# Gates of a retrieval layer as two float16 pieces instead of three bf16 ones, and kept in DRAM with eight keys side by side instead of four

## The chip, the cores and the metric

The kernel runs on one core of a Trainium2 chip. Its time is the device time of one launch in microseconds. The engines of the core are named as the profile names them: PE (TensorE, matmuls; PEld is its weight load), DVE (VectorE), ACT (ScalarE), POOL (GpSimd), SP (the queue that issues most DMAs). Each of them works through its own list of instructions in order and waits on semaphores that the others set.

## What is computed

The reference is one decoder block on 512 tokens of width 1024: a mixer (a recurrent group of heads beside sliding-window attention), then a layer that retrieves experts, then a final norm. The change touches the retrieval layer only. Cut to what matters:

```python
def block(x_b):                                  # x_b: a block of tokens, h after the norm
    q = (x_b @ wq).reshape(-1, H, 2, PEER_HALF)  # 8 heads, two half queries
    s = einsum('thcd,hcnd->thcn', q, subkeys)    # 128 scores for each half
    s_top, i_top = top_k(s, 16)
    cand_s = s_top[:, :, 0, :, None] + s_top[:, :, 1, None, :]
    cand_i = i_top[:, :, 0, :, None] * 128 + i_top[:, :, 1, None, :]
    best_s, best_pos = top_k(cand_s, 16)
    idx = take(cand_i, best_pos)                 # 8 x 16 experts for a token
    gate = softmax(best_s)
    act = gelu(einsum('td,ted->te', x_b, u_tab[idx]))
    return einsum('te,ted->td', gate * act, v_tab[idx])
```

There are 128 x 128 experts, each named by a pair of keys.

## The kernel before

**Two ways for the tokens.** The first 128 tokens gather their 128 expert rows each from the tables (indirect DMAs on POOL, line 1079; the dot products and sums on DVE, lines 1092 and 1090). The other 384 tokens (ND) are done densely: for each of 128 blocks b (one value of one key; the 128 values of the other key lie on the partitions) the kernel multiplies all 128 experts of the block with all 384 tokens (`up_product`, 24 matmuls of 384 columns at lines 173 to 175, since every operand is split into a high and a low part), takes the Gelu (`up_act`, line 886), multiplies by a dense matrix of gates that is zero where an expert was not chosen (`weigh`, line 1218, on POOL) and adds the product with the block's value rows into six PSUM banks (`accumulate`, lines 1263 to 1265).

**The gates.** The dense gates are made ahead of the main loop, in 96 steps n of four tokens each, 8 steps to a group of TC = 32 tokens, 32 steps to a tile of 128 tokens. At the start of a tile `chosen(t)` transposes the gates and both keys of the 128 chosen slots (line 1109), copies the gates to `rest` (1115) and the keys to `sK` (1117), and takes the gates apart into bf16 pieces `sG`: a cast on ACT (1119), and between two casts a subtraction on DVE (1121), three casts and two subtractions. For each step `one_hots(n)`, called three steps ahead, makes on DVE the tile `O` (1136: for four tokens the one-hot rows of both keys, 1024 elements) and `P` (1141: the one-hot row of one key times each of the three pieces, 1536 elements). PE then multiplies O with P (1163): for each of four tokens three matmuls of 128 columns, added up in PSUM as `pG`. ACT copies `pG` to the staging tile `gst` (1164). After 8 steps one DMA writes `gst`, 2 MB, to DRAM (`gates`, 1173). In DRAM a partition's GI x TC numbers for GI = 4 blocks b lie side by side, 512 bytes; the last group of 32 tokens is written in eight parts (1173 and 1242).

**What else lies between.** A fixed order is written out by hand (`manual_schedule`): during the 96 steps the program also runs 34 `up_product`s ahead (each in two halves, by `steps(ups, ...)`), with `up_split` (a cast on ACT, line 163, and a subtraction on DVE, line 164, that make `uh` and `ul`), the load of the next `u` block (`up_load`, 783), and 44 of the gathers with their DVE work. Then, after the last gates are written, `gate_load` (1202) reads the gates back, 12 DMAs of 64 KB for four blocks b, and the main loop over 128 blocks begins.

Of the kernel before, what the change touches and what calls it, by code (L numbers as in the profile page):

```python
# [6 lines left out]

F32 = mybir.dt.float32
F32R = mybir.dt.float32r
BF = mybir.dt.bfloat16  # L10
I32 = mybir.dt.int32
U32 = mybir.dt.uint32
AF = mybir.ActivationFunctionType
# [33 lines left out]
AHEAD = 2  # L47

LASTG = 120
ND = 384  # L50
CH0 = 512 - ND
NCAND = [min(16, 16 // (a + 1)) for a in range(16)]
# [21 lines left out]
def _emit(ctx, tc, A, out, dbg, stop):  # L74
    nc = tc.nc
    V, SC, PE, GP, SY = nc.vector, nc.scalar, nc.tensor, nc.gpsimd, nc.sync
    mm = PE.matmul
# [109 lines left out]
    def pt(tag, name, shape=(128, 512)):  # L187
        return ps.tile(list(shape), F32, name=name, tag=tag, bufs=2)
# [16 lines left out]
    def rms(pool, n, width, name, add_eng):  # L205


        acc = pool.tile([128, S], F32, name=name + "acc")
        rs = consts.tile([128, NT], F32, name=name + "rs")

        def take(k, src):
            if k == 0:
                SC.activation(acc, src, AF.Square)
                return
            sq = pool.tile([128, S], F32, name=name + "sq", tag="rsq", bufs=3)
            SC.activation(sq, src, AF.Square)
            (V if k == n - 1 else add_eng).tensor_tensor(out=acc, in0=acc, in1=sq, op=OP.add)

        def scale():
            pss = pt("att", name + "ss", (128, NT))  # L220
            for t in range(NT):
                mm(pss[:, t:t + 1], acc[:, t * 128:(t + 1) * 128], ones[:, 0:1], start=True, stop=True)
            rsqrt(rs, pss, NT, 1.0 / width, RMS_EPS)
            return rs

        def spread():
            pb = pt("att", name + "b")
            for t in range(NT):
                mm(pb[:, t * 128:(t + 1) * 128], rs[:, t:t + 1].to_broadcast([128, 128]), ident,
                   start=True, stop=True)  # L230
            return pb

        return take, scale, spread


    take, scale, spread = rms(xp, KD, D, "n1", V)
# [528 lines left out]
    mpst, mp = right("mp")  # L765
# [4 lines left out]
    iota = mp.tile([128, 128], F32, name="iota")  # L770
    GP.iota(iota, pattern=[[1, 128]], base=0, channel_multiplier=0, allow_small_or_imprecise_dtypes=True)

    iota2 = mp.tile([128, 128, 2], BF, name="iota2")
    GP.iota(iota2, pattern=[[1, 128], [0, 2]], base=0, channel_multiplier=0, allow_small_or_imprecise_dtypes=True)

    pust, pool_u = right("pu", 2)
# [37 lines left out]
    take, scale, spread = rms(x2p, KD, D, "n2", GP)  # L814
    for i in range(KD):
        whi, wlo = load_w(A["w_out"][i])
        p = pt(("proj", "chain")[i % 2], "pj")
# [27 lines left out]
    for k in range(KD):  # L845
        p = pt("tinv", "px2", (128, NT, 128))
# [67 lines left out]
    tk = tkst.enter_context(tc.tile_pool(name="tk", bufs=1, side="right", reuse_waits="tile"))  # L914
# [113 lines left out]
    for hc in range(16):  # L1028
# [8 lines left out]
        p = psT.tile([128, 512], F32, name="pq", tag="pq", bufs=2)  # L1037
# [5 lines left out]
        p = psT.tile([128, NT, 128], F32, name="psc", tag="psc", bufs=2)  # L1043
# [26 lines left out]
    tk = tkst.enter_context(tc.tile_pool(name="oh", bufs=1, side="right", reuse_waits="tile"))  # L1070
# [12 lines left out]
    def gathered(j):  # L1083
# [7 lines left out]
        else:  # L1091
            V.scalar_tensor_tensor(scr, r_, 1.0, h2g, op0=OP.mult, op1=OP.mult, accum_out=ac[:, jj:jj + 1])  # L1092

    TC, GI = 32, 4
    NG = 128 // GI
    NTC = ND // TC

    NG0 = 4
    gd = [[nc.dram_tensor(f"gates{t}_{g0}", (n, 128, GI * TC), F32, kind="Internal").ap() for g0, n in
           (((0, NG0), (NG0, NG - NG0)) if t == NTC - 1 else ((0, NG),))] for t in range(NTC)]  # L1100
    hot = {}

    def chosen(t):

        sK = tk.tile([128, 64, 2, 2], BF, name="sK", tag="sK", bufs=2)
        sG = tk.tile([128, 64, 3, 2], BF, name="sG", tag="sG", bufs=2)
        p = psT.tile([128, 3, 128], F32, name="psT", tag="sel", bufs=2)
        for i in range(3):
            PE.transpose(p[:, i, :], sg_[:, i, t].rearrange("p h s -> p (h s)"), ident)
        rest = tk.tile([128, 64, 2], F32, name="rest", tag="rest")  # L1110

        def pairs(x):
            return x.rearrange("p (n t) -> p n t", t=2)

        SC.copy(rest, pairs(p[:, 0]))
        for i in range(2):
            SC.copy(sK[:, :, i], pairs(p[:, 1 + i]))
        for i in range(3):
            SC.copy(sG[:, :, i], rest)
            if i < 2:  # L1120
                V.tensor_tensor(out=rest, in0=rest, in1=sG[:, :, i], op=OP.subtract)
        hot["s"] = sK, sG

    def one_hots(n):

        t, t0 = CH0 // 128 + n // 32, n % 32 * 4
        if t >= NT:
            return
        if t0 == 0:
            chosen(t)  # L1130
        sK, sG = hot["s"]
        ts = slice(t0 // 2, t0 // 2 + 2)

        O = tk.tile([128, 2, 2, 256], BF, name="O", tag="O", bufs=3)
        P = tk.tile([128, 2, 3, 256], BF, name="P", tag="P", bufs=3)
        V.tensor_tensor(out=O.rearrange("p n i (e t) -> p (n i) e t", t=2),  # L1136
                        in0=iota2[:, None].to_broadcast([128, 4, 128, 2]),
                        in1=sK[:, ts].rearrange("p n i t -> p (n i) t")[:, :, None, :].to_broadcast([128, 4, 128, 2]),
                        op=OP.is_equal)
        B5 = [128, 2, 3, 128, 2]  # L1140
        V.tensor_tensor(out=P.rearrange("p n i (e t) -> p n i e t", t=2),  # L1141
                        in0=O[:, :, 1:2].rearrange("p n i (e t) -> p n i e t", t=2).to_broadcast(B5),
                        in1=sG[:, ts, :, None, :].to_broadcast(B5), op=OP.mult)
        hot[n] = [x.rearrange("p n i (e t) -> p n i e t", t=2) for x in (O, P)]

    V.scalar_tensor_tensor(h2g, x2[:, 0, :], rs2[:, 0:1], ln2r, op0=OP.mult, op1=OP.mult)
    for n in range(3):
        one_hots(n)
    def pieces(ci):
        return ([(0, NG0)] + [(g, 4) for g in range(NG0, NG, 4)]) if ci == NTC - 1 else [(0, NG)]  # L1150

    done = asked = 0
    left = 2 * len(AHEAD_UP) - sum(UPS1) - sum(UPST) - BEHIND
    for n in range(8 * NTC):
        one_hots(n + 3)
        O, P = hot.pop(n)
        ci, t4 = n // 8, n % 8
        if t4 == 0:
            gst = tk.tile([128, NG, GI, TC], F32, name="gst", tag="gst", bufs=2)
        p = psT.tile([128, 4, 128], F32, name="pG", tag=("sel", "pq", "psc")[n % 3], bufs=2)  # L1160
        for u in range(4):
            for i in range(3):
                mm(p[:, u, :], O[:, u // 2, 0, :, u % 2], P[:, u // 2, i, :, u % 2], start=i == 0, stop=i == 2)  # L1163
        SC.copy(gst[:, :, :, t4 * 4:t4 * 4 + 4].rearrange("p n g t -> p (n g) t"), p.rearrange("p t e -> p e t"))  # L1164
        if t4 == 7:

            writes = []
            for g0, n_ in pieces(ci):
                d = gd[ci][g0 >= NG0 and ci == NTC - 1]
                d0 = NG0 if d.shape[0] == NG - NG0 else 0  # L1170
                writes.append((d[g0 - d0:g0 - d0 + n_].rearrange("n p x -> p n x"),
                               gst[:, g0:g0 + n_].rearrange("p n g t -> p n (g t)")))
            SY.dma_start(*writes.pop(0))
        steps(ups, (n + 1) * left // (8 * NTC) - n * left // (8 * NTC))
        while asked < (n + 1) * EARLY // (8 * NTC):
# [16 lines left out]
    def upto(b):  # L1192

        return min(256, EARLY + (256 - EARLY) * sum(cost[:b + 1]) // sum(cost[:LASTG + 1]))

    vs, ws, gts = {}, {}, {}

    def gate_load(g):
        gts[g] = pv_.tile([128, NTC, GI, TC], F32, name="gts", tag="gts", bufs=2)
        for i in range(NTC):  # L1200
            d, n = (gd[i][0], g) if len(gd[i]) == 1 or g < NG0 else (gd[i][1], g - NG0)
            SY.dma_start(gts[g][:, i], d[n].rearrange("p (g t) -> p g t", t=TC))  # L1202

    def load(b):
        if b >= 128:
# [86 lines left out]
    for b in range(127):  # L1292
# [10 lines left out]
        n = RING + b  # L1303
# [11 lines left out]
        for j in range(done, n1):  # L1315
            gather(j)
        if b > LASTG:
            steps(ends[0], 1)
# [74 lines left out]
```

## Time and profile before

| | |
|---|---|
| median of 3 runs | 1682.41 us (1679.21 to 1683.79) |
| the profiled execution's own time | 1679.72 us |
| its span | 1678.0 us |
| PE busy | 1607.2 us, 96% |
| DVE busy | 1305.7 us, 78% |
| ACT busy | 656.5 us, 39% |
| POOL busy | 712.4 us, 42% |
| the 96 gate steps | from about 601 us to 844 us of the span |

The span is the time from the first to the last instruction of the profiled execution; 1.7 us of its time lie around it. The busy times are unions of an engine's instructions; the end of a matmul is modelled, so a busy PE may still be waiting for a few ns in between. A row of a group gives how many instructions it holds, their busy time, the mean length of one, and the idle time ahead of them with what ended it.

### The profile page before, as it was taken

What the parts mean: (1) busy time and instruction counts of PE and PEld (TensorE: products, weight loads), DVE (VectorE), ACT (ScalarE), POOL (GpSimd) and SP (SyncE); (2) the same over time, 40 slices, a digit from 0 to 9 for tenths busy, and PEclk for the clock granted to TensorE, in tenths of its full rate; (3) what the DMA queues carried; (4) which work ended last, traced back from release to release, by engine and by line L of the source; (5) the groups of instructions that cost most, each with busy time, mean ns of one, the idle gap of its engine ahead of it and who ended that gap; (6) DMA issues with size and microseconds to landing.
All of it is one profiled execution on the core that took longest, in us unless ns stands there. A gap on an engine that the chain in (4) does not pass through costs nothing.

```text
span 1678.0 us, 30955 instructions
## 1 busy us (share of the span) xinstructions
PE 1607.2 (96%) x12013; PEld 1386.1 (83%) x12013; DVE 1305.7 (78%) x2477; ACT 656.5 (39%) x1081; POOL 712.4 (42%) x670
## 2 busy tenths in 40 slices
PE   5999999898999989989999999999999999999997
PEld 4777677676888889888889888888888888888886
DVE  5656448745799889999958777877878877788797
ACT  5444345533343434444443333333333333333334
POOL 5112110034676512121216565556565556556582
PEclk9999999999999999999999999999999999999999
DMA  4111110141222249898989989989888989889784
GB/s 133 52 40 41 53 59 2 63 157 63 79 98 101 101 148 306 288 324 285 306 310 360 322 305 324 321 307 326 303 321 303 318 294 344 308 298 338 255 301 152
DMA packets 204692, 369.62 MB, mean 220 GB/s; under 512 B 17792, under 2 KB 126848, under 8 KB 204288
## 3 DMA queue, kind: packets, MB, share of 16 engines
q1 hardware_dynamic: 161632, 225.14, 39.5%
q0 software_dynamic: 36864, 134.23, 22.3%
q10 hardware_dynamic: 6048, 8.26, 1.3%
q8 instruction: 94, 1.54, 0.4%
q14 instruction: 54, 0.44, 0.1%
HBM read 332.04 MB, written 35.52 MB: 219 GB/s over the span
## 4 chain that ended last, share of the span: by engine, by line
PE 51%; DVE 12%; issue 2%; ACT 1%; DMA 1%; SPq 0%; POOL 0%; DVEq 0%; ACTq 0%; POOLq 0%
PE acc L1263 10%; PE acc L1265 10%; PE acc L1264 10%; PE pA L173 7%; PE pA L175 7%; PE pA L174 7%; DVE P L1141 3%; DVE O L1136 3%; DVE scr L1092 3%; DVE ul L164 2%; PE pG L1163 0%; DMA u<-in_uT_dram 0%; SPq L1202 0%; ACT uh L163 0%; DVE x L1287 0%
## 5 line engine op out<-in xcount | busy, mean ns | idle before, releaser
L175 PE MATMUL pA<-h2hi,ul 128*128 128x384 f32 x1024 | 349.4, 341 | 10.7 <-DVE ul L164 7.0
L173 PE MATMUL pA<-h2hi,uh 128*128 128x384 f32 x1024 | 355.1, 347 | 3.6 <-ACT actd L886 2.0
L174 PE MATMUL pA<-h2lo,uh 128*128 128x384 f32 x1024 | 347.6, 339 | 0.0
L1079 POOL DMA_INDIRECT row<-in_u_dram,ix x128 | 175.6, 1372 | 315.1 <-DVE scr L1092 274.2
L1263 PE MATMUL acc<-vh,wh 128*128 128x512 f32 x768 | 299.5, 390 | 1.3 <-ACT vh L163 1.3
L1265 PE MATMUL acc<-vl,wh 128*128 128x512 f32 x768 | 299.0, 389 | 0.8 <-DVE vl L164 0.8
L1264 PE MATMUL acc<-vh,wl 128*128 128x512 f32 x768 | 299.3, 390 | 0.0
L1079 POOL DMA_INDIRECT row<-in_vB_dram,ix x128 | 195.0, 1523 | 142.3 <-DVE x L1090 119.2
L164 DVE TENSOR_TENSOR vl<-v,vh 128x1024 fp32r<-128x1024 f32 x128 | 217.3, 1698 | 36.0 <-ACT vh L163 32.8
L175 PEld LDWEIGHTS pA<-h2hi,ul 128*128 128x128 f32 x1024 | 194.1, 190 | 15.3 <-DVE ul L164 10.9
L173 PEld LDWEIGHTS pA<-h2hi,uh 128*128 128x128 f32 x1024 | 194.2, 190 | 7.4 <-ACT actd L886 2.2
L174 PEld LDWEIGHTS pA<-h2lo,uh 128*128 128x128 f32 x1024 | 194.2, 190 | 3.0
L1090 DVE SCALAR_TENSOR_TENSOR x<-row,ac,x 128x1024 f32<-128x1024 f32 x128 | 173.0, 1351 | 4.5 <-DMA row<-in_vB_dram,ix 2.6
L1265 PEld LDWEIGHTS acc<-vl,wh 128*128 128x128 f32 x768 | 144.2, 188 | 32.0 <-DVE vl L164 1.4
L1263 PEld LDWEIGHTS acc<-vh,wh 128*128 128x128 f32 x768 | 144.2, 188 | 29.2 <-ACT vh L163 1.6
L1264 PEld LDWEIGHTS acc<-vh,wl 128*128 128x128 f32 x768 | 144.1, 188 | 27.4
L1092 DVE SCALAR_TENSOR_TENSOR scr<-row,h2g 128x1024 f32<-128x1024 f32 x128 | 157.4, 1230 | 2.2 <-DMA row<-in_u_dram,ix 0.9
L163 ACT CAST uh<-u 128x1024 fp32r<-128x1024 f32 x128 | 134.2, 1049 | 63.4 <-PE pA L174 33.0
L164 DVE TENSOR_TENSOR ul<-u,uh 128x1024 fp32r<-128x1024 f32 x109 | 134.9, 1238 | 20.9 <-ACT uh L163 17.6
L163 ACT CAST vh<-v 128x1024 fp32r<-128x1024 f32 x128 | 134.0, 1047 | 0.1
L1164 ACT COPY gst<-pG 128x512 f32<-128x512 f32 x96 | 55.9, 587 | 122.6 <-PE pG L1163 117.4
L1141 DVE TENSOR_TENSOR P<-O,sG 128x1536 bf16<-128x1536 bf16 x96 | 92.0, 958 | 3.5
(711 smaller groups left out, 2530.0 us busy)
## 6 DMA issues: line engine op xcount, KB each, us to landing
u<-in_uT_dram SPq DMA_DIRECT2D x128, 512.0 KB
v<-in_vB_dram SPq DMA_DIRECT2D x128, 512.0 KB
gts<-gates SPq DMA_DIRECT2D x384, 64.0 KB
gates<-gst SPq DMA_DIRECT2D x11, 2048.0 KB
w<-in_w_in_dram SPq DMA_DIRECT2D x40, 256.0 KB
wq<-in_wq_dram SPq DMA_DIRECT2D x16, 512.0 KB
acts<-actd ACTq DMA_DIRECT2D x42, 192.0 KB
act<-acts SPq DMA_DIRECT2D x42, 192.0 KB
```

Of the source, the lines that this page charges most:

```text
L163: (hi_eng or SC.copy)(dst_hi, src)
L164: (lo_eng or V).tensor_tensor(out=dst_lo, in0=src, in1=dst_hi.bitcast(F32), op=OP.subtract)
L173: mm(ps, whi[k][:, :m], ahi[:, k], start=k == 0, stop=False)
L174: mm(ps, whi[k][:, :m], alo[:, k], start=False, stop=False)
L175: mm(ps, wlo[k][:, :m], ahi[:, k], start=False, stop=k == KD - 1)
L1079: GP.indirect_dma_start(r_, None, A["vB"].rearrange("b p d -> (b p) d") if w_ else A["u"], bass.IndirectOffsetOnAxis(ap=ix[:, w_, jj:jj + ...
L1090: V.scalar_tensor_tensor(x2[:, 0, :], r_, ac[:, jj:jj + 1], x2[:, 0, :], op0=OP.mult, op1=OP.add)
L1092: V.scalar_tensor_tensor(scr, r_, 1.0, h2g, op0=OP.mult, op1=OP.mult, accum_out=ac[:, jj:jj + 1])
L1141: V.tensor_tensor(out=P.rearrange("p n i (e t) -> p n i e t", t=2), in0=O[:, :, 1:2].rearrange("p n i (e t) -> p n i e t", t=2).to_broadca ...
L1263: mm(o, wh[:, ts], vh[:, ds_], start=b == 0, stop=False)
L1264: mm(o, wl[:, ts], vh[:, ds_], start=False, stop=False)
L1265: mm(o, wh[:, ts], vl[:, ds_], start=False, stop=b == 127)
```

## The change

The gates are multiplied by GS = 32768 when they leave the transpose, taken apart into two float16 pieces (two casts and one subtraction) and divided by GS again when `pG` goes to `gst`; both scalings ride on copies on ACT that were there before, now written as an activation with the function Copy. The one-hot tiles are float16, `P` has 1024 elements instead of 1536, and each token takes two matmuls instead of three. In DRAM the gates of GW = 8 blocks lie side by side (1024 bytes of a partition), so each `gate_load` of four blocks reads one half of each such row; `n`, the number of eights, and `part`, which half, are worked out in `gate_load`. The eight parts of the last write hold as many blocks each as before. Every other line stays.

```diff
+GS = 32768.0
...
-    iota2 = mp.tile([128, 128, 2], BF, name="iota2")
+    iota2 = mp.tile([128, 128, 2], HF, name="iota2")
...
-    TC, GI = 32, 4
-    NG = 128 // GI
+
+    TC, GI, GW = 32, 4, 8
+    NG = 128 // GW
     NTC = ND // TC
 
-    NG0 = 4
-    gd = [[nc.dram_tensor(f"gates{t}_{g0}", (n, 128, GI * TC), F32, kind="Internal").ap() for g0, n in
+    NG0 = 2
+    gd = [[nc.dram_tensor(f"gates{t}_{g0}", (n, 128, GW * TC), F32, kind="Internal").ap() for g0, n in
...
-        sK = tk.tile([128, 64, 2, 2], BF, name="sK", tag="sK", bufs=2)
-        sG = tk.tile([128, 64, 3, 2], BF, name="sG", tag="sG", bufs=2)
+
+        sK = tk.tile([128, 64, 2, 2], HF, name="sK", tag="sK", bufs=2)
+        sG = tk.tile([128, 64, 2, 2], HF, name="sG", tag="sG", bufs=2)
...
-        SC.copy(rest, pairs(p[:, 0]))
+        SC.activation(rest, pairs(p[:, 0]), AF.Copy, scale=GS)
         for i in range(2):
             SC.copy(sK[:, :, i], pairs(p[:, 1 + i]))
-        for i in range(3):
+        for i in range(2):
             SC.copy(sG[:, :, i], rest)
-            if i < 2:
+            if i < 1:
                 V.tensor_tensor(out=rest, in0=rest, in1=sG[:, :, i], op=OP.subtract)
...
-        O = tk.tile([128, 2, 2, 256], BF, name="O", tag="O", bufs=3)
-        P = tk.tile([128, 2, 3, 256], BF, name="P", tag="P", bufs=3)
+        O = tk.tile([128, 2, 2, 256], HF, name="O", tag="O", bufs=3)
+        P = tk.tile([128, 2, 2, 256], HF, name="P", tag="P", bufs=3)
...
-        return ([(0, NG0)] + [(g, 4) for g in range(NG0, NG, 4)]) if ci == NTC - 1 else [(0, NG)]
+        return ([(0, NG0)] + [(g, 2) for g in range(NG0, NG, 2)]) if ci == NTC - 1 else [(0, NG)]
...
         for u in range(4):
-            for i in range(3):
-                mm(p[:, u, :], O[:, u // 2, 0, :, u % 2], P[:, u // 2, i, :, u % 2], start=i == 0, stop=i == 2)
-        SC.copy(gst[:, :, :, t4 * 4:t4 * 4 + 4].rearrange("p n g t -> p (n g) t"), p.rearrange("p t e -> p e t"))
+            for i in range(2):
+                mm(p[:, u, :], O[:, u // 2, 0, :, u % 2], P[:, u // 2, i, :, u % 2], start=i == 0, stop=i == 1)
+        SC.activation(gst[:, :, :, t4 * 4:t4 * 4 + 4].rearrange("p n g t -> p (n g) t"),
+                      p.rearrange("p t e -> p e t"), AF.Copy, scale=1.0 / GS)
...
-            d, n = (gd[i][0], g) if len(gd[i]) == 1 or g < NG0 else (gd[i][1], g - NG0)
-            SY.dma_start(gts[g][:, i], d[n].rearrange("p (g t) -> p g t", t=TC))
+            n, part = g // (GW // GI), g % (GW // GI)
+            d, n = (gd[i][0], n) if len(gd[i]) == 1 or n < NG0 else (gd[i][1], n - NG0)
+            SY.dma_start(gts[g][:, i], d[n, :, part * GI * TC:(part + 1) * GI * TC].rearrange("p (g t) -> p g t", t=TC))
```

No instruction changes its place among its neighbours. On DVE, at the second tile of tokens (`scr` is the dot product of a gathered row, `ul` the low part of a loaded block), before:

```order
L1136 TENSOR_TENSOR O<-iota_4465,sK 128x1024
L1141 TENSOR_TENSOR P<-O,sG 128x1536
L1092 SCALAR_TENSOR_TENSOR scr,ac<-row,h2g 128x1024
L1121 TENSOR_TENSOR rest<-rest,sG 128x128 x2
L1136 TENSOR_TENSOR O<-iota_4465,sK 128x1024
L1141 TENSOR_TENSOR P<-O,sG 128x1536
L164 TENSOR_TENSOR ul<-u,uh 128x1024
```

and now:

```order
L1140 TENSOR_TENSOR O<-iota_4465,sK 128x1024
L1145 TENSOR_TENSOR P<-O,sG 128x1024
L1094 SCALAR_TENSOR_TENSOR scr,ac<-row,h2g 128x1024
L1125 TENSOR_TENSOR rest<-rest,sG 128x128
L1140 TENSOR_TENSOR O<-iota_4465,sK 128x1024
L1145 TENSOR_TENSOR P<-O,sG 128x1024
L166 TENSOR_TENSOR ul<-u,uh 128x1024
```

The list is the same with a shorter P and one subtraction for two. On ACT, at the same place (`actd` is the Gelu of a block that goes to DRAM), before:

```order
L1115 COPY rest<-psT 128x128
L1117 CAST sK<-psT 128x64x2 x2
L1119 CAST sG<-rest 128x64x2 x3
L1164 COPY gst<-pG 128x128x4
L163 CAST uh<-u 128x1024
L886 ACTIVATE actd<-pA 128x384
```

and now:

```order
L1119 ACTIVATE rest<-psT 128x128
L1121 CAST sK<-psT 128x64x2 x2
L1123 CAST sG<-rest 128x64x2 x2
L1168 ACTIVATE gst<-pG 128x128x4
L165 CAST uh<-u 128x1024
L888 ACTIVATE actd<-pA 128x384
```

The copies have become activations, one cast is gone, and no load of a function table stands between the activation of `gst` and that of `actd`.

## Rows read from the trace of the kernel before

**Rows 1.** The view by windows: for four stretches their length, then busy us and instructions of PE, PEld, DVE, ACT and POOL, the granted clock of PE, the DMA share and GB/s.

```profile
606.00:628.00 22.00, 21.84 (x187) 20.70 (x185) 20.12 (x25) 9.31 (x15) 1.85 (x2) 0.89 0.46 158
628.00:842.00 214.00, 200.02 (x1767) 183.92 (x1765) 210.08 (x280) 94.41 (x160) 43.98 (x39) 0.99 0.90 303
842.00:870.00 28.00, 27.41 (x164) 26.93 (x162) 11.41 (x13) 9.10 (x14) 3.88 (x5) 1.00 0.87 280
870.00:1640.00 770.00, 768.51 (x3737) 682.12 (x3738) 615.78 (x609) 272.55 (x375) 453.92 (x334) 1.00 0.90 314
```

**Rows 2.** The view of waits from 628 to 842 us, PE's own: who waited for whom, us in total, times, the longest.

```profile
PE pG L1163 <- DVE P L1141: 6.3, 13, 0.7
PE pA L175 <- DVE ul L164: 5.6, 6, 1.3
```

**Rows 3.** The timeline of DVE from 659.4 to 668.4 us: start, length, engine, line.

```profile
662.25 0.69 DVE L1136 TENSOR_TENSOR O<-iota,sK 128x1024 bf16<-128x1024 bf16 x1
662.98 0.96 DVE L1141 TENSOR_TENSOR P<-O,sG 128x1536 bf16<-128x1536 bf16 x1
663.86 0.68 DVE L1136 TENSOR_TENSOR O<-iota,sK 128x1024 bf16<-128x1024 bf16 x1
664.57 0.96 DVE L1141 TENSOR_TENSOR P<-O,sG 128x1536 bf16<-128x1536 bf16 x1
665.45 1.22 DVE L164 TENSOR_TENSOR ul<-u,uh 128x1024 fp32r<-128x1024 f32 x1
666.59 1.22 DVE L1092 SCALAR_TENSOR_TENSOR scr<-row,h2g 128x1024 f32<-128x1024 f32 x1
```

**Rows 4.** Groups of instructions by line and shape from 600 to 845 us: how many, busy us, mean ns of one, idle time ahead.

```profile
L1141 DVE TENSOR_TENSOR P<-O,sG 128x1536 bf16<-128x1536 bf16 x96 | 92.0, 958 | 3.5
L1163 PE MATMUL pG<-P,O 128*128 128x128 bf16 x1152 | 82.1, 221 | 10.4 <-DVE P L1141 10.3
...
L1136 DVE TENSOR_TENSOR O<-iota,sK 128x1024 bf16<-128x1024 bf16 x96 | 65.8, 686 | 1.5 <-PE pG L1163 1.5
L1164 ACT COPY gst<-pG 128x512 f32<-128x512 f32 x96 | 55.9, 587 | 122.6 <-PE pG L1163 117.4 <-issue 3.0 <-ACT actd L886 1.2
...
L1121 DVE TENSOR_TENSOR rest<-rest,sG 128x128 f32<-128x128 f32 x6 | 1.7, 289 | 1.1 <-ACT sG L1119 1.1
```

**Rows 5.** The view by windows for line 1141 (P) on DVE alone: the stretch, its busy us and instructions, clock, DMA share, GB/s.

```profile
628.00:842.00 214.00, 79.74 (x84) 0.99 0.90 303
```

**Rows 6.** The timeline of PE from 660 to 676 us: the twelve matmuls of a gate step and the first of the product behind them; then the three transposes (f32, 128 columns) of a new tile and the step behind them.

```profile
663.99 0.86 PE L1163 MATMUL pG<-P,O 128*128 128x128 bf16 x12 [0.65 <-DVE P L1141]
...
664.66 0.42 PE L173 MATMUL pA<-h2hi,uh 128*128 128x384 f32 x1
...
673.29 0.50 PE L1109 MATMUL psT<-ident,sg__4943 128*128 128x128 f32 x3
...
673.62 0.85 PE L1163 MATMUL pG<-P,O 128*128 128x128 bf16 x12
```

**Rows 7.** Groups of ACT over the whole span: activations of 128x512 numbers from PSUM with a constant scale (L316) and with a scale out of a tile (L291).

```profile
L291 ACT ACTIVATE pm<-pj,c__162 128x512 f32<-128x512 f32 (+1 forms) x14 | 9.7, 692 | 0.0
...
L316 ACT ACTIVATE ld<-pld 128x512 f32<-128x512 f32 x4 | 2.4, 595 | 1.4 <-PE pld L315 1.3
```

**Rows 8.** The view of line 886 (the Gelu) over the whole span, its loads of a function table: how many, ns shortest/median/longest, first and last start in us.

```profile
L886 ACT ACT_TABLE_LOAD  x5: 1283/1283/1283, 427.4 to 573.7; - x5
```

**Rows 9.** The view of DMA from 600 to 845 us: queue, packets, MB, share of the 16 engines' time; then issues with KB each. Queue 0 carries the gathered rows, queue 10 `acts` (1.5 KB of a partition), queue 1 all that SP issues.

```profile
q1 hardware_dynamic: 49992, 40.39, 52.4%
q0 software_dynamic: 6167, 22.48, 24.4%
q10 hardware_dynamic: 4896, 6.69, 7.4%
...
gates<-gst SPq DMA_DIRECT2D x11, 2048.0 KB
u<-in_uT_dram SPq DMA_DIRECT2D x32, 512.0 KB
...
gates<-gst SPq DMA_DIRECT2D x1, 256.0 KB
```

**Rows 10.** The timeline of SP from 600 to 845 us: one write of gates and the three loads of `u` issued behind it.

```profile
661.12 0.38 SPq L1173 DMA_DIRECT2D gates<-gst  x1
661.60 8.05 SPq L783 DMA_DIRECT2D u<-in_uT_dram  x3
```

**Rows 11.** The timeline of PE from 858 to 884 us: matmuls at the start of the main loop, with PE's idle time ahead of them.

```profile
870.66 0.50 PE L1263 MATMUL acc<-vh,wh 128*128 128x512 f32 x1 [1.26 <-ACT vh L163]
...
872.22 0.50 PE L1265 MATMUL acc<-vl,wh 128*128 128x512 f32 x1 [0.82 <-DVE vl L164]
```

**Rows 12.** The chain of waits from 836 to 900 us, two of its pieces at the end of the stage: start, length, what.

```profile
853.81 6.46 DMA u<-in_uT_dram
...
864.86 1.93 DMA gts<-gates
```

**Rows 13.** The view of DMA from 880 to 1640 us, as rows 9.

```profile
q1 hardware_dynamic: 84551, 127.52, 48.5%
q0 software_dynamic: 30201, 110.00, 40.8%
...
gts<-gates SPq DMA_DIRECT2D x365, 64.0 KB
```

More of the change, by code (lines that the diff above doesn't have):

```diff
@@ L9 @@
 F32R = mybir.dt.float32r
-BF = mybir.dt.bfloat16
+HF = mybir.dt.float16
 I32 = mybir.dt.int32
@@ L1139, in one_hots @@
                         op=OP.is_equal)
-        B5 = [128, 2, 3, 128, 2]
+        B5 = [128, 2, 2, 128, 2]
         V.tensor_tensor(out=P.rearrange("p n i (e t) -> p n i e t", t=2),
@@ L1158, in _emit @@
         if t4 == 0:
-            gst = tk.tile([128, NG, GI, TC], F32, name="gst", tag="gst", bufs=2)
+            gst = tk.tile([128, NG, GW, TC], F32, name="gst", tag="gst", bufs=2)
         p = psT.tile([128, 4, 128], F32, name="pG", tag=("sel", "pq", "psc")[n % 3], bufs=2)
         for u in range(4):
-            for i in range(3):
-                mm(p[:, u, :], O[:, u // 2, 0, :, u % 2], P[:, u // 2, i, :, u % 2], start=i == 0, stop=i == 2)
-        SC.copy(gst[:, :, :, t4 * 4:t4 * 4 + 4].rearrange("p n g t -> p (n g) t"), p.rearrange("p t e -> p e t"))
+            for i in range(2):
+                mm(p[:, u, :], O[:, u // 2, 0, :, u % 2], P[:, u // 2, i, :, u % 2], start=i == 0, stop=i == 1)
+        SC.activation(gst[:, :, :, t4 * 4:t4 * 4 + 4].rearrange("p n g t -> p (n g) t"),
+                      p.rearrange("p t e -> p e t"), AF.Copy, scale=1.0 / GS)
         if t4 == 7:
```

## The prediction

> **What bounds the kernel now.** I read the windows first [rows 1], to see which engine has no time left in which part. From 870 us on PE is busy for 768.5 of 770 us; nothing that makes gates runs there. The change can work only in the gate stage, from 601 to about 870 us. In the 214 us from 628 to 842 us DVE is busy for 210.1 us, PE for 200.0 us and ACT for 94.4 us, and the DMA engines show a share of 0.90. So DVE binds, PE stands 5% behind it and DMA not far behind that. The waits say the same: PE waits for P for 6.3 us and for the low parts `ul` for 5.6 us, both of them DVE's work [rows 2]. Before 628 us PE is the full one (21.84 of 22 us), and from 842 us on PE again (27.41 of 28 us), working off the products that the program kept back [rows 1].
>
> **DVE, the bound.** In the timeline an O starts and 0.72 us later its P, and 0.88 us after the P the next instruction starts [rows 3]; a gate step costs 1.60 us there, and O and P lie back to back with other work behind them. P goes from 1536 elements to 1024. That is the shape of O, also a two-input instruction over 16-bit tiles: 686 ns against 958 ns [rows 4], so P gets 272 ns shorter. In the DVE-bound stretch lie 84 P [rows 5]: 84 x 0.272 = **22.8 us**. The subtraction at line 1121: six of them cost 1.7 us and 1.1 us of waiting for the cast between them [rows 4]; three remain and the casts between pairs go, so 2.0 us go for three tiles, two of them inside the stretch: **1.3 us**. The other 0.7 us go at the start, before the first P, where nothing hides them.
>
> No row shows float16 on DVE. The near ends are O at 686 ns (16-bit) and the subtraction `ul` over 1024 f32 elements at 1.22 us [rows 3]. I take the 16-bit end, since the element size is the same as O's before; the other end is a rival below. There is no lower end: with the shape of O, a P below O's 686 ns would need a rate that no row has.
>
> The Trainium skill, "Advanced Engine Details and Errata", section 2x-1p Requirements, names both BF16 and FP16 among the data types of the mode with two elements a cycle; no run here shows FP16. By it the sum stays, and the rival on float16 below is small.
>
> **PE, second.** Twelve matmuls of a step start at 663.99 us and the next product at 664.66 us [rows 6]: 56 ns each. Four fewer a step are 0.22 us, in the stretch 84 x 0.22 = 18.8 us, so PE's 200.0 us become 181.2 us while DVE's 210.1 become 186.0 us. PE was at 95% of DVE's work and is at 97%; it stays second, and I expect its small waits for DVE to stay about what they are. A matmul in float16 is in no row; the ends are 56 ns (bf16) and 0.33 us / 3 = 0.11 us (the f32 transposes of the same 128 columns, 673.29 to 673.62 us [rows 6]). At the far end the stretch's 84 x 8 matmuls would cost 36 us more and PE would bind, at 217 us, no better than now. I take 56 ns, by element size. In the 22 us before 628 PE binds, and some 10 steps give 10 x 0.22 = 2.2 us; with the 0.7 us at the start **2.9 us**. After the last P only one step's 0.22 us is left, **0.2 us**.
>
> **ACT, covered.** The copy of pG takes 587 ns [rows 4]. As an activation over 128x512 from PSUM with a constant scale it is nearest to 595 ns, with a scale from a tile 692 ns [rows 7]: 0.8 us over 96 steps, at most 10 us. ACT has 120 of 214 us free [rows 1], which hides both ends; only the 0.1 us at most by which one pG leaves later would show, once, at the end. The function Copy could bring loads of a table between Copy and Gelu, 1.283 us each; the trace shows none on the Gelu's line behind 573.7 us [rows 8], and the order of the changed kernel has no load between `gst` and `actd`. Cost 0.
>
> **DMA, third.** The same 25 MB of gates go to DRAM in rows of 1024 instead of 512 bytes. What the rows of 512 bytes cost follows by taking the rest away [rows 9]: gathered rows take 24.4% / 22.48 MB = 1.085% a MB, `acts` 7.4 / 6.69 = 1.106%. The 32 loads of `u` (16.8 MB) at 1.085 are 18.2%, and 34.2% of queue 1 are left for the gates' 23.3 MB: 1.47% a MB, and a little less since one small load is also in queue 1; I use 1.45. So the small rows cost a third more than others. For 1024 bytes the ends are 1.45 (nothing gained) and 1.106 (rows of 1.5 KB); I take 1.2, near the latter, which is the nearest in size: 23.3 x 0.25 = 5.8% of 245 us = 14 us of DMA time less. In the stretch 0.90 x 214 = 193 us of DMA time become some 180 us, to be done in 214 - 24 = 190 us: a share of 0.95. That is above the 0.90 at which the main loop runs with PE full [rows 1], so some of it may show. SP's loads of `u` are issued behind each write of gates and take 8.05 us for three [rows 10]; the fewer rows of a write can only shorten that. I put **2 us** on waits for `u` that grow.
>
> A rule of the Trainium skill speaks against this half of the change: "DMA: Bandwidth & Descriptors", section Specifications, gives 512 bytes as the least transfer for line rate. By that rule the rows of 512 bytes are at line rate already, 1024 bytes save no DMA time, and the first rival below decides more often. The trace disagrees, 1.45 against 1.09% a MB.
>
> **The end of the stage.** PE runs out of products and waits 1.26 and 0.82 us before the main loop [rows 11], behind a chain of a load of `u` (6.46 us) and the first gates read back (1.93 us) [rows 12]. Writes that cost less could win these 2.1 us; reads that take half of each 1024-byte row could cost as much. I put 0, with 2 us either way.
>
> **The sum.** 22.8 + 1.3 + 2.9 + 0.2 - 2 = 25.2 us. The profiled execution takes 1679.7 us (span 1678.0), so 1654.5 us; it lies 2.7 us under the median of the runs shown, 1682.4, which gives 1657.2. I say **1657 us**.
>
> **Rivals.** *DMA takes over.* If rows of 1024 bytes cost what those of 512 did, 193 us of DMA time have to fit the stretch. The main loop holds 0.90 over 770 us [rows 1]; how far above that DMA can be driven no row tells, and I estimate 0.96: 193 / 0.96 = 201 us instead of 190. The saving falls from 25 to 14 us: 1668 us. For it: DMA is third already. Against it: the price of the small rows.
>
> *float16 is slow on DVE (slower than before).* If it goes at the f32 rate, O and P cost 1.14 us each from start to start, as `ul` does [rows 3], 2.28 us a step instead of 1.60: 0.68 x 96 = 65 us more, some 60 with the parts where DVE had room: 1742 us. It decides from the point at which O and P together pass 1.60 us; if P alone is slow (0.72 + 1.14 = 1.86), it is 25 us, 1707 us. For it: no row has float16. Against it: O and P move at 0.53 ns an element ((958 - 686) / 512), the f32 `ul` at 1.05 ((1220 - 142) / 1024, with the 142 ns that O has beside its elements); the half goes with the half element size, which float16 shares.
>
> *The main loop starves.* The 365 reads of 64 KB (23.9 MB) are 48.5% less 103.6 MB at 40.8 / 110 = 0.371% a MB, so 10.1%, or 0.42% a MB [rows 13]. If reading halves of rows doubled that, DMA's share of the main loop would go from 0.90 to 1.00; at 0.96 the 770 us become 802, and the whole comes out at 1657 + 32 = 1689 us. For it: PE's 100% there rest on DMA at 0.90. Against it: each read still lands as 512 bytes on a partition, as before.
>
> *The end gives its 2 us and no `u` is late.* Saving 29 to 32 us, 1651 us.
>
> **How the numbers follow.** The forecast, 1653 to 1662 us, has 0.68; DMA takes over 0.17; the main loop starves 0.04; float16 slow 0.03; the end gives more 0.08. The range of 1650 to 1670 us takes in the first, the second and the last but for their edges. About 0.3%, 5 us, is what a measurement of this kernel can tell from no change. Faster than that: 0.68 + 0.17 + 0.08, less a little of the second, 0.92. Slower: 0.03 + 0.02 of the starving loop, 0.05. The same: 0.03.
>
> **What would show it.** P at about 686 ns with 96 in number; 768 matmuls of pG at 56 ns from one to the next; DVE still busy for 98% of a stretch that has become some 24 us shorter, PE's waits still for P and `ul`. The DMA view of the stage with half the packets for the gates and queue 1's share of time down from its 52.4% of 245 us (128 us) to about 114 us. The main loop as long as now, PE full in it. I am wrong if ACT waits for `u` add up to more than some 5 us (DMA took over), if O or P is at 1.2 us, or if PE has idle time after 870 us.

## The result, and the profile after

The changed kernel takes 1652.7 us (median of 4 runs, 1651.63 to 1654.51) where the kernel before, on the same chip, takes 1681.45 (1679.21 to 1683.79): a ratio of 0.983 with a 95% interval of 0.981 to 0.984. That is 28.8 us less; 25.2 were forecast. The profiled execution's own time is 1651.63 us, its span 1649.9.

The windows of the changed kernel, with the columns of [rows 1]. The stretches are cut where the same work begins and ends:

```profile
606.00:628.00 22.00, 22.00 (x176) 20.87 (x174) 20.54 (x29) 11.57 (x19) 2.17 (x2) 0.97 0.64 222
628.00:816.00 188.00, 176.99 (x1404) 160.23 (x1403) 184.62 (x274) 90.28 (x154) 43.80 (x38) 1.00 0.95 339
816.00:843.00 27.00, 26.08 (x146) 25.32 (x145) 11.00 (x12) 10.64 (x15) 4.93 (x5) 1.00 0.90 306
843.00:1612.00 769.00, 768.28 (x3736) 681.98 (x3736) 615.01 (x608) 270.90 (x373) 454.10 (x333) 1.00 0.90 314
```

DVE is busy for 98% of the gate stage, as before, and the stage is some 26 us shorter. DVE itself waits for others for 0.4 us in the whole stretch from 628 to 816 us. The DMA share has gone from 0.90 to 0.95. The main loop is PE's as before, 768.28 of 769 us, with the DMA share at the same 0.90.

The groups by line from 600 to 820 us, which answer to [rows 4]:

```profile
L1145 DVE TENSOR_TENSOR P<-O,sG 128x1024 f16<-128x1024 f16 x96 | 66.4, 692 | 3.5
L1140 DVE TENSOR_TENSOR O<-iota,sK 128x1024 f16<-128x1024 f16 x96 | 65.7, 685 | 0.9 <-PE pG L1167 0.9
L1167 PE MATMUL pG<-P,O 128*128 128x128 f16 x768 | 59.5, 222 | 7.7 <-DVE P L1145 7.6
L1168 ACT ACTIVATE gst<-pG 128x512 f32<-128x512 f32 x96 | 55.9, 597 | 100.6 <-PE pG L1167 98.8 <-ACT actd L888 1.6
...
L1125 DVE TENSOR_TENSOR rest<-rest,sG 128x128 f32<-128x128 f32 x3 | 0.9, 284 | 0.0
```

P went from 958 to 692 ns, 6 ns above the 686 that were taken for it. O as float16 is where it was as bf16. There are 768 matmuls of `pG`, the copy to `gst` takes 597 ns instead of 587, and of the subtractions with their 1.1 us of waiting three are left, with none.

PE's waits from 628 to 816 us, which answer to [rows 2], and below them ACT's waits for `u` from 600 to 820 us (who waited for whom, us in total, times, the longest):

```profile
PE pA L177 <- DVE ul L166: 4.7, 6, 1.3
PE pG L1167 <- DVE P L1145: 4.4, 10, 0.5
PE pA L175 <- ACT actd L888: 1.4, 1, 1.4
...
ACT uh L165 <- DMA u<-in_uT_dram: 3.6, 2, 2.8
```

PE still waits for DVE and for nothing else of weight. ACT waits for a load of `u` twice, for 3.6 us, and PE doesn't feel it.

A gate step in the timeline of DVE from 640 to 645 us (start, length, engine, line), as [rows 3], and its matmuls in that of PE, as [rows 6]:

```profile
641.14 0.69 DVE L1145 TENSOR_TENSOR P<-O,sG 128x1024 f16<-128x1024 f16 x1
641.75 0.69 DVE L1140 TENSOR_TENSOR O<-iota,sK 128x1024 f16<-128x1024 f16 x1
642.47 0.69 DVE L1145 TENSOR_TENSOR P<-O,sG 128x1024 f16<-128x1024 f16 x1
643.08 1.22 DVE L1094 SCALAR_TENSOR_TENSOR scr<-row,h2g 128x1024 f32<-128x1024 f32 x1
...
642.70 0.63 PE L1167 MATMUL pG<-P,O 128*128 128x128 f16 x8
643.14 0.42 PE L175 MATMUL pA<-h2hi,uh 128*128 128x384 f32 x1
```

From O to its P it is 0.72 us as before, from the P to the next instruction 0.61 instead of 0.88: a step costs DVE 1.33 us instead of 1.60. On PE eight matmuls take 0.44 us, 55 ns each.

DMA from 600 to 818 us, as [rows 9], and in the timeline of SP one write of gates with the loads of `u` behind it, as [rows 10]:

```profile
q1 hardware_dynamic: 27598, 40.52, 54.0%
q0 software_dynamic: 6192, 22.55, 27.4%
q10 hardware_dynamic: 4896, 6.69, 8.6%
...
653.08 0.38 SPq L1178 DMA_DIRECT2D gates<-gst  x1
653.56 5.55 SPq L785 DMA_DIRECT2D u<-in_uT_dram  x3
```

Queue 1 moves the same 40 MB with little more than half the packets, in 54.0% of 218 us, 118 us of DMA time against 128 before. The three loads behind a write are issued in 5.55 us, not 8.05.

The view of the tile `pG`, before and now: how many matmuls, ns shortest/median/longest, first and last start in us.

```profile
L1163 PE MATMUL pG<-P,O x1152: 217/218/308, 605.2 to 843.9; 128*128 128x128 bf16 x192
L1167 PE MATMUL pG<-P,O x768: 217/218/312, 603.9 to 815.7; 128*128 128x128 f16 x192
```

**Where the time went.** The last `pG` matmul starts at 815.7 us instead of 843.9, 28.2 us earlier; from there to the first matmul of the main loop it is 26.2 us instead of 26.8; from that to the end of the span 808.0 instead of 807.3. In sum 28.2 + 0.6 - 0.7 = 28.1 us, the difference of the spans. Of the 28.2 us, 26.9 lie between the first and the last `pG` (211.8 us instead of 238.7): that is the gate stage. The other 1.3 lie ahead of the first `pG`, and the runs below whose code is the same up to there start it anywhere from 603.2 us (e6) to 606.7 us (e11), so this part can't be told from chance.

### The profile page after: what moved, and what is told of

It is laid out like the page before. It is cut to its first block, busy times and chain, and to the rows that moved or that the text cites. A ratio compares the mean times of both kernels' runs of the same rounds, so it can differ in the third digit from the quotient of the medians.

```text
span 1649.9 us, 30181 instructions
## 1 busy us (share of the span) xinstructions
PE 1584.4 (96%) x11629; PEld 1362.9 (83%) x11629; DVE 1279.5 (78%) x2474; ACT 655.2 (40%) x1078; POOL 712.3 (43%) x670
## 4 chain that ended last, share of the span: by engine, by line
PE 49%; DVE 11%; DMA 3%; issue 2%; ACT 1%; SPq 0%; POOL 0%; DVEq 0%; POOLq 0%; ACTq 0%
PE acc L1271 10%; PE acc L1269 10%; PE acc L1270 10%; PE pA L177 7%; PE pA L175 7%; PE pA L176 7%; DVE O L1140 3%; DVE ul L166 2%; DVE scr L1094 2%; DVE P L1145 2%; DMA u<-in_uT_dram 1%; DMA row<-in_vB_dram,ix 0%; DMA gts<-gates 0%; DMA acts<-actd 0%; PE pG L1167 0%
## 5 line engine op out<-in xcount | busy, mean ns | idle before, releaser
L1270 PEld LDWEIGHTS acc<-vh,wl 128*128 128x128 f32 x768 | 144.1, 188 | 27.4
L1168 ACT ACTIVATE gst<-pG 128x512 f32<-128x512 f32 x96 | 55.9, 597 | 100.6 <-PE pG L1167 98.8
L888 ACT ACTIVATE act<-pA 128x384 f32<-128x384 f32 x86 | 42.2, 491 | 132.6 <-PE pA L177 132.6
```

Of the source, the lines that this page charges most:

```text
L1168: SC.activation(gst[:, :, :, t4 * 4:t4 * 4 + 4].rearrange("p n g t -> p (n g) t"), p.rearrange("p t e -> p e t"), AF.Copy, scale=1.0 / GS)
L1270: mm(o, wl[:, ts], vh[:, ds_], start=False, stop=False)
```

## The experiments

The theory is the prediction's: DVE sets the stage, the shorter P makes the gain, and the wider rows only keep DMA from taking the bound. Its rivals: the rows make a part of the gain by themselves; the four matmuls that PE is spared make it; float16 matters for its rate. The runs e1 to e5 change one thing each to tell these apart; the other six ask whether still wider rows help, what stands behind DVE, and whether a better version exists. The ratios are against the kernel before, run beside each, with 95% intervals.

| run | edit | median us | ratio |
|---|---|---|---|
| e1 | the change without the wide rows | 1657.05 | 0.985 [0.984, 0.987] |
| e2 | the wide rows alone | 1680.61 | 0.999 [0.999, 1.000] |
| e3 | PE spared, DVE not | 1679.79 | 0.999 [0.998, 1.000] |
| e4 | DVE spared, PE not | 1662.29 | 0.989 [0.987, 0.990] |
| e5 | two bf16 pieces | 1652.93 | 0.982 [0.981, 0.983] |
| e6 | a third of the `ul` on POOL | 1662.65 | 0.988 [0.987, 0.990] |
| e7 | e6, rows of 2048 bytes | 1665.81 | 0.989 [0.988, 0.991] |
| e8 | rows of 2048 bytes | 1652.19 | 0.982 [0.981, 0.984] |
| e9 | 36 early gathers, not 44 | 1648.85 | 0.980 [0.979, 0.982] |
| e10 | 26 early gathers | 1641.54 | 0.976 [0.974, 0.977] |
| e11 | 10 early gathers | 1639.61 | 0.974 [0.973, 0.976] |

Every diff below is against the changed kernel, but for that of e2.

### The rows: e1 and e2

```diff
-    TC, GI, GW = 32, 4, 8
+    TC, GI, GW = 32, 4, 4
-    NG0 = 2
+    NG0 = 4
-        ... [(0, NG0)] + [(g, 2) for g in range(NG0, NG, 2)] ...
+        ... [(0, NG0)] + [(g, 4) for g in range(NG0, NG, 4)] ...
```

> Two float16 pieces as in the change, but rows of 512 bytes in DRAM as before (four blocks side by side). If DVE's shorter work is the gain and DMA has room: as the changed kernel, 1651 to 1656 us. If the wide rows are needed to make that room (193 us of DMA time in a stretch of 188): 1657 to 1665 us, with ACT waiting for u for more than 10 us. If the wide rows are the gain itself: 1676 us or more.

Without the wide rows the kernel takes 1657.05 us, 4.3 us more than with them; the two were measured apart, but their ranges don't meet (1655.99 to 1658.55 and 1651.63 to 1654.51). Its gate stage in the view by windows, and DMA from 600 to 822 us:

```profile
628.00:820.00 192.00, 179.79 (x1424) 162.56 (x1422) 186.98 (x276) 91.73 (x156) 43.74 (x38) 1.00 0.99 335
...
q1 hardware_dynamic: 50415, 41.00, 57.9%
```

The DMA share is 0.99. Queue 1 needs 57.9% of 222 us, 129 us against 118 with the rows of 1024 bytes, some 10 us of it for the same gates. The rule of the Trainium skill that the prediction weighed ("DMA: Bandwidth & Descriptors", section Specifications: line rate from 512 bytes on) would have both cost the same; the trace disagrees. ACT's waits for `u` from 600 to 850 us, here and (second line) in the changed kernel:

```profile
ACT uh L165 <- DMA u<-in_uT_dram: 20.8, 10, 4.9
...
ACT uh L165 <- DMA u<-in_uT_dram: 7.2, 3, 3.6
```

Most of that doesn't reach PE: ACT waits 13.6 us longer for `u`, while PE's own waits from 628 to 860 us add up to 14.7 us against 11.9. What the trace of e1 has more is 1.9 us in the stage, from the first to the last `pG` (213.7 us against 211.8, which e5 and e8 repeat within 0.1), and 2.5 us between it and the main loop (28.7 against 26.2), where the chain of waits of e1 from 790 to 860 us runs over three loads of `u`, and PE stands still (start, length, what; then PE's timeline):

```profile
802.86 11.94 DMA u<-in_uT_dram
...
820.87 9.20 DMA u<-in_uT_dram
...
831.66 6.53 DMA u<-in_uT_dram
...
848.23 0.80 PE L1269 MATMUL acc<-vh,wh 128*128 128x512 f32 x1 [3.15 <-ACT vh L165]
```

e2 puts the wide rows into the kernel before: three bf16 pieces, with `GW = 8` for the tiles in DRAM, the staging tile and the reads as in the change.

```diff
-    TC, GI = 32, 4
-    NG = 128 // GI
+    TC, GI, GW = 32, 4, 8
+    NG = 128 // GW
-    NG0 = 4
+    NG0 = 2
...
+            n, part = g // (GW // GI), g % (GW // GI)
```

> Three bf16 pieces as before, but rows of 1024 bytes. If DVE binds the stage: as the kernel before, 1679 to 1684 us, with the DMA share of 628 to 842 us down from 0.90 to about 0.84. If the rows make the gain: 1655 to 1670 us.

1680.61 us against 1682.12 of the kernel before, which can't be told from no change. Its gate stage:

```profile
628.00:842.00 214.00, 198.98 (x1766) 182.59 (x1765) 210.08 (x281) 93.50 (x159) 44.45 (x39) 1.00 0.87 302
```

The DMA share falls from 0.90 to 0.87, less than the 0.84 that was expected, and DVE is busy for the same 210.08 us [rows 1]. So the rows give DMA time, and time to the kernel only once DVE's work is shorter. They don't make the gain; they keep 4.3 us of it.

### DVE's part and PE's part: e3 and e4

e3 gives DVE its old work and leaves PE its new one: three float16 pieces are made, the third is multiplied into P, and no matmul uses it.

```diff
-        sG = tk.tile([128, 64, 2, 2], HF, name="sG", tag="sG", bufs=2)
+        sG = tk.tile([128, 64, 3, 2], HF, name="sG", tag="sG", bufs=2)
-        for i in range(2):
+        for i in range(3):
             SC.copy(sG[:, :, i], rest)
-            if i < 1:
+            if i < 2:
...
-        P = tk.tile([128, 2, 2, 256], HF, name="P", tag="P", bufs=3)
+        P = tk.tile([128, 2, 3, 256], HF, name="P", tag="P", bufs=3)
...
-        B5 = [128, 2, 2, 128, 2]
+        B5 = [128, 2, 3, 128, 2]
```

> The changed kernel, but DVE makes P with three float16 pieces (1536 elements, two subtractions) of which PE multiplies only the first two; the third, a rest of the gates that is next to nothing, is left out of the product. If DVE's work sets the time: its 25.5 + 2 us come back, 1676 to 1682 us. If the four matmuls fewer in a step set it: 1651 to 1657 us.

1679.79 us: all but 2 us of the gain is gone. The stage by windows, and PE's waits in it:

```profile
628.00:840.00 212.00, 183.09 (x1405) 163.01 (x1404) 208.12 (x277) 92.90 (x159) 43.15 (x38) 0.98 0.88 303
...
PE pG L1167 <- DVE P L1145: 16.5, 19, 1.6
PE pA L177 <- DVE ul L166: 8.7, 6, 1.8
```

PE has lost its matmuls and stands idle instead: 25.2 us of waits for P and `ul` where the kernel before has 11.9 [rows 2]. DVE is at 98% of the stretch.

e4 is the other half: DVE makes two pieces, and PE does three matmuls a token, the second piece twice (so the low parts count double).

```diff
-            for i in range(2):
-                mm(p[:, u, :], O[...], P[:, u // 2, i, :, u % 2], start=i == 0, stop=i == 1)
+            for i in range(3):
+                mm(p[:, u, :], O[...], P[:, u // 2, min(i, 1), :, u % 2], start=i == 0, stop=i == 2)
```

> The changed kernel with DVE's two pieces, but PE does three matmuls for a token, the second piece twice, so the gates' low part counts double. PE's work in the stretch of 188 us rises from 177 to 196 us and passes DVE's 185. If DVE alone counted, whatever PE does: 1651 to 1656 us. If the longer of the two sets the time: 8 to 14 us more than the changed kernel, 1660 to 1667 us. If PE's matmuls were the gain: 1676 us or more.

The stage by windows, and the view of `pG` as above:

```profile
628.00:824.00 196.00, 196.00 (x1789) 185.90 (x1789) 189.77 (x281) 95.43 (x160) 45.60 (x40) 1.00 0.94 334
...
L1167 PE MATMUL pG<-P,O x1152: 217/218/308, 606.0 to 822.6; 128*128 128x128 f16 x192
```

1662.29 us: 19.8 us of the gain stay and 9.6 are lost. PE is busy for all 196 us of the stretch and waits for nothing. In the trace, taken of the shortest execution (1658.21 us), the stage is 216.6 us from the first to the last `pG`, 4.8 more than the changed kernel's; where the slower executions lose the rest was not seen. So sparing PE alone gives 2 us at most, and sparing DVE alone stops where PE binds; the whole gain needs both.

### float16 against bf16: e5

```diff
-HF = mybir.dt.float16
+HF = mybir.dt.bfloat16
```

> The changed kernel with bf16 in place of float16 everywhere (two bf16 pieces, so the gates keep fewer digits). If the type costs nothing and only the number of pieces counts: as the changed kernel, 1651 to 1655 us, P at 686 to 692 ns, a matmul of pG at 56 ns. If float16 is slower or faster than bf16 on DVE or PE: O or P off by more than 10 ns, 1 us or more for each 10 ns.

The gates keep fewer digits in two bf16 pieces; all else is the same. Groups by line from 600 to 820 us:

```profile
L1145 DVE TENSOR_TENSOR P<-O,sG 128x1024 bf16<-128x1024 bf16 x96 | 66.4, 692 | 3.5
...
L1167 PE MATMUL pG<-P,O 128*128 128x128 bf16 x768 | 59.5, 221 | 7.7 <-DVE P L1145 7.2 <-issue 0.4
```

1652.93 us, 692 ns and 221 ns: nothing differs by more than 1 ns or 0.3 us. float16 costs and gains no time on either engine; it is there for the digits of the gates, which no time shows.

### A faster DVE, tried by moving work to POOL: e6 and e7

```diff
-        split(uh, ul, us.pop(b), lo_eng=GP if 0 < b < 20 else V)
+        split(uh, ul, us.pop(b), lo_eng=GP if 0 < b < 20 or b in SPILL[::3] else V)
```

> The changed kernel, but of the blocks run ahead every third one that goes to DRAM has its low part ul made on POOL instead of DVE: some 12 of 35 in the stage, 12 x 1.14 = 14 us less for DVE (185 to 171 us of 188). If DVE alone sets the time: 14 us less, 1639 us. If PE (177 us) is right behind: 5 to 8 us less, 1645 to 1648 us, PE busy 99%. If DMA (share 0.95) is: 2 to 6 us less, 1647 to 1651 us, with ACT waiting for u. If POOL's slower subtraction (2.4 us) comes late for PE: 1652 us or more, with PE waiting for POOL's ul.

If DVE binds and POOL is idle for three quarters of the stage, a third of the `ul` moved to POOL should help. It took 1662.65 us, 10 us more than the changed kernel. That lies in the last of the expected cases, but its reason, PE waiting for POOL's `ul`, is the smaller part: PE does so for 3.0 us in all. The groups by line from 600 to 825 us, and DVE and POOL in one stretch of the timeline:

```profile
L1145 DVE TENSOR_TENSOR P<-O,sG 128x1024 f16<-128x1024 f16 x96 | 80.9, 843 | 3.5
L1140 DVE TENSOR_TENSOR O<-iota,sK 128x1024 f16<-128x1024 f16 x96 | 74.3, 774 | 1.7 <-PE pG L1167 1.6
...
L166 POOL TENSOR_TENSOR ul<-u,uh 128x1024 fp32r<-128x1024 f32 x11 | 28.8, 2623 | 57.0 <-ACT uh L165 52.0 <-PE pG L1167 5.0
...
650.99 2.58 POOL L166 TENSOR_TENSOR ul<-u,uh 128x1024 fp32r<-128x1024 f32 x1 [3.81 <-ACT uh L165]
...
651.33 2.78 DVE L1145 TENSOR_TENSOR P<-O,sG 128x1024 f16<-128x1024 f16 x1
...
654.74 0.69 DVE L1145 TENSOR_TENSOR P<-O,sG 128x1024 f16<-128x1024 f16 x1
```

O and P have become 23.1 us longer in sum, and that not evenly: a P that runs while POOL subtracts takes 2.78 us, and the next one 0.69 again. It ends 0.54 us after POOL's instruction does (653.57 us), about as though it had begun only then. All ten subtractions on POOL from 628 to 820 us have one such O or P beside them, of 2.75 to 3.15 us, and no other O or P there is longer than 0.72 us. The Trainium skill, "SBUF — State Buffer", section "SBUF: two separate sides", tells of a port pair that DVE and GpSimd share as a lock held for a whole instruction, by a DVE operation with two SBUF inputs against a GpSimd operation that reads SBUF. The trace agrees. A subtraction moved to POOL saves DVE 1.14 us and costs it 2.1, 2.78 - 0.69. Eleven of them save 12.5 us, so with the 23.1 us DVE has 10.6 us more to do; from the first to the last `pG` the stage is 222.5 us (603.2 to 825.7) instead of 211.8, 10.7 us longer.

e7 is e6 with `GW = 16`, rows of 2048 bytes, in case DMA held e6 back.

> As the run before, and the gates in rows of 2048 bytes (16 blocks side by side). If DMA holds that run back: 2 to 5 us less than it. If PE does: within 1.5 us of it.

1665.81 us, 3.2 more than e6 with ranges that overlap, so neither of the two expected cases, and no better: it wasn't DMA.

### Still wider rows: e8

```diff
-    TC, GI, GW = 32, 4, 8
+    TC, GI, GW = 32, 4, 16
-    NG0 = 2
+    NG0 = 1
-        ... [(0, NG0)] + [(g, 2) for g in range(NG0, NG, 2)] ...
+        ... [(0, NG0)] + [(g, 1) for g in range(NG0, NG)] ...
```

> The changed kernel with rows of 2048 bytes, nothing else. If DVE sets the time and DMA has room: within 1.5 us of the changed kernel, 1651 to 1654 us, DMA's share of 628 to 816 us down to about 0.92. If DMA still costs something at 1024 bytes: 2 to 4 us less. If reading quarters of rows costs the main loop: 2 us or more above, with PE idle after 843 us.

1652.19 us, which can't be told from 1652.7, and a DMA share of 0.94 in the stage instead of 0.95, where 0.92 was expected. At 1024 bytes the rows have given what they have to give.

### Less of DVE's other work in the stage: e9, e10, e11

```diff
-EARLY = 44
+EARLY = 36
```

> The changed kernel, but 36 instead of 44 gathers of the first tile stand in the gate stage; the other eight move to the main loop, where DVE is busy 615 of 769 us. DVE loses 8 x 1.14 = 9 us in the stage (185 to 176 us of 188, PE 177), DMA 4.2 MB or 11 us. If the longest engine sets the time: 5 to 8 us less than the changed kernel, 1645 to 1648 us, with PE and DVE both near 98%. If the main loop can't take the gathers (DMA at 0.90 there): the gain is lost behind 843 us, 1651 us or more, with PE idle there. If DVE didn't bind any more: 1651 to 1654 us.

`EARLY` says how many of the 256 gathers, each with 1.14 us of DVE's time, are done during the gate steps; the rest go to the main loop, where DVE is busy for 80%. At 36 the kernel takes 1648.85 us, 3.9 less than at 44, a little short of what was expected. Eight gathers are 9 us of DVE's time, but also 4.2 MB of DMA, so this run alone doesn't part the two. What speaks for DVE is that PE's waits in the changed kernel are for DVE, that DVE waits for nothing there but 0.4 us for ACT, and that a small relief of DMA alone, e8, gave nothing.

e10 sets `EARLY = 26` and e11 `EARLY = 10`.

> As the run before with 26 gathers in the stage: DVE at 164 us, well below PE's 177. If PE is the next bound: no more than 2 us below the run with 36. If DVE went on setting the time: 10 us below it. If the main loop fills: above it.

> The changed kernel with 10 gathers in the gate stage instead of 44. With 26 PE was busy 178.9 of 180 us from 628 to 808 us and waited 1 us for DVE. If PE is the bound there: the stage gets no shorter (first to last matmul of pG 196 to 199 us), and the main loop grows by 1 to 3 us for 16 more gathers, so 1641 to 1645 us. If DVE still set a part: 3 us or more below the run with 26. If the main loop is full (DMA 0.93 there): 1648 us or more, with PE idle in it.

26 gives 1641.54 us, 7.3 less than 36, where at most 2 had been expected; 10 gives 1639.61, just below the 1641 to 1645 expected with PE as the bound. The gate stage by windows for e9, e10 and e11:

```profile
628.00:808.00 180.00, 173.43 (x1383) 158.68 (x1382) 174.73 (x257) 89.93 (x154) 35.23 (x31) 1.00 0.93 327
```

```profile
628.00:808.00 180.00, 178.91 (x1453) 167.22 (x1452) 170.79 (x246) 92.46 (x160) 25.73 (x22) 1.00 0.92 313
```

```profile
628.00:808.00 180.00, 180.00 (x1466) 169.83 (x1465) 156.28 (x216) 94.90 (x162) 6.87 (x6) 1.00 0.82 273
```

The view of `pG` for e11:

```profile
L1167 PE MATMUL pG<-P,O x768: 217/218/309, 606.7 to 802.4; 128*128 128x128 f16 x192
```

PE's busy time rises from 173 to 180 of 180 us while DVE's falls. From the first to the last `pG` matmul it is 211.8 us at 44, 206.0 at 36, 198.1 at 26 and 195.7 at 10: DVE binds down to about 26, and from there PE does. e11 beats both kernels, by 2.6% and 0.8%; e10 lies 2 us above it, which can't be told from no difference, since the ranges overlap (1637.47 to 1642.43 and 1640.82 to 1642.31).

## Why the prediction was right, and where its sizes were off

**The time: in the range, near its lower end.** 1652.7 us lies in 1650 to 1670, and 0.3 us below the 1653 to 1662 that the forecast held likeliest. Of the 4.5 us to the 1657.2 of the sum, 2.9 are terms of the stage and its end, below; 1.6 are the step from the profiled execution to the median, 2.7 us before and 1.1 now.

**DVE binds, and P's length is the gain: right.** P came out at 692 ns, 266 ns shorter instead of 272, so the term of 22.8 us is 22.3 by that row. e3 takes the gain back with DVE's work alone.

**PE stays second: right, but nearer was said than it is.** The prediction put PE at 97% of DVE's work, from busy times. e11, in which PE is busy for every microsecond from 628 to 808, needs 195.7 us where the changed kernel takes 211.8: PE's work is 92% of the stage, and DVE is busy for 98% of it, so PE is at 94% of DVE. e4, with the twelve matmuls a step of the kernel before, says the same of that kernel: 216.6 of 238.7 us, 91%, where PE was busy for 93% (200.02 of 214 us [rows 1]). A part of the difference can be seen in PE's timeline above: eight `pG` are listed until 643.33 us (642.70 + 0.63), though the next matmul starts at 643.14, so a listed end reaches up to 0.2 us into a wait behind it. The Trainium skill, "Perfetto Trace Analysis", section "Identifying the Most-Contended Engine", calls the matmuls' busy share no good measure of how close PE is to its roofline and names the weight loads' busy share as one to use instead. The traces agree for the kernel before: PEld is at 86% (183.92 of 214 us) and in e4 at 95% (185.90 of 196), a ratio of 0.91, as 216.6 to 238.7. For the changed kernel neither share is on the mark of 0.92: PEld against that of e11 gives 0.90 (160.23 of 188 and 169.83 of 180), PE's busy share 0.94. None of this touched the sum, since DVE bound either way, but it misled the expectation for e10.

**The gate stage's terms, 22.8 + 1.3 + 2.9 + 0.2 = 27.2 us: right to 1 us.** The last `pG` is 28.2 us earlier. All but 0.7 of the 27.2 were to lie behind the first `pG`, 26.5, and 26.9 do. The 0.7 stand against the 1.3 us ahead of it, which chance alone can give.

**The 2 us for waits for `u`: the term that was mis-sized.** The DMA share rose to 0.95 as worked out, and the gates' price came close to the value chosen: queue 1's 118 us less some 47 for the loads of `u` (17.3 MB at queue 0's 27.4% x 218 / 22.55 = 2.65 us a MB) and a small load leave 70.5 us for 23.6 MB, 1.22% of 245 us a MB where 1.2 was taken, a choice between two ends that fell well. (Queue 1 is at 118 us and not at the 114 forecast since its window holds one load of `u` and one write more.) But ACT waits only 0.9 us longer for `u` than before, 3.6 us against the 2.7 of this row from 600 to 845 us:

```profile
ACT uh L163 <- DMA u<-in_uT_dram: 2.7, 2, 2.2
```

A third wait, 3.6 us at the start of the main loop, was there before as well (3.55 us). In the stage none of PE's waits follows from a late `u`. ACT is idle for half of the stage, which hides these waits; in e1 even 20.8 us of them went with a loss of 4.3.

**The end of the stage, 0: nearly right.** PE waits 0.56 and 0.82 us before the main loop instead of 1.26 and 0.82 [rows 11]: PE's timeline has

```profile
841.90 0.50 PE L1269 MATMUL acc<-vh,wh 128*128 128x512 f32 x1 [0.56 <-ACT vh L165]
...
843.46 0.50 PE L1271 MATMUL acc<-vl,wh 128*128 128x512 f32 x1 [0.82 <-DVE vl L166]
```

That gives 0.6 us, and the chain of waits there still holds a load of `u`, now 6.64 us long [rows 12]. With the 2 us not lost, the 1 us more of the stage and this, less 0.7 us in the main loop, the sum of 25.2 becomes the 28.1 of the spans.

**The rivals.** *DMA takes over*: its condition, small rows, is e1, and the stage is then at a share of 0.99, above the 0.96 that was estimated as the most; the price was 4.3 us, not 11. With the rows of the change it decides nothing. *float16 is slow* fell with P's row and e5. *The main loop starves* fell: PE's 768.28 of 769 us, at the same DMA share. *The end gives its 2 us and no `u` is late*, 1651 us, came nearest in size: no `u` was late for PE, though the end gave only 0.6.

## What to carry to other kernels

When the bounding engine is to be relieved, price the engine behind it by a run in which that one never waits: its busy time in a stage with many short waits overstates its work. Here the busy times put PE 8 us below DVE (176.99 against 184.62), and 16 us lay between them, most of which moving gathers out of the stage then gave. Wider rows in DRAM were worth nothing here while DVE bound (e2), and paid 4.3 us when the stage had shrunk onto the same transfers (e1); so the two edits belong together, and each alone says little of the pair. Work that two engines could take isn't moved for free: look at what the receiving engine's instruction does to its neighbour's before counting the saved time.

## What the runs showed of the hardware

A two-input operation of DVE over 16-bit tiles (0.69 us) took 2.78 us beside a subtraction on POOL of 2.58 us, and ended after it; it was so beside each of the ten subtractions on POOL from 628 to 820 us (e6).

The same gates cost queue 1 some 10 us less DMA time in rows of 1024 bytes than in rows of 512 (118 us against 129, e1), and rows of 2048 bytes brought the share from 0.95 to 0.94 only (e8).

In e1 PE waits 3.15 us before the main loop. The granted clock behind the wait was 0.50, the level of 1.2 GHz, and the first matmul took 0.80 us instead of 0.50:

```profile
845.00:848.20 3.20, 0.08 (x1) 0.00 (x0) 1.95 (x2) 2.07 (x3) 2.56 (x4) 1.00 0.99 393
848.20:851.40 3.20, 3.06 (x6) 1.99 (x7) 3.20 (x3) 1.04 (x1) 2.14 (x2) 0.50 1.02 413
```

In the changed kernel, where PE waits 0.56 and 0.82 us at the same place, the clock stays at 1.00. So a part of e1's loss may be the clock after the wait and not the wait itself; it is a small one, since from the first matmul of the main loop to the end e1 takes 808.6 us and the changed kernel 808.0.
